# Weight pieces of the MoE experts as halves of one matrix, four rows in one run on each partition; x1, residual and output in natural column order

## The chip, the cores and the metric

The kernel runs on one core of a Trainium2 chip. The metric is the device time of one execution in microseconds (us), the median over several executions. Times below that are not this median come from one profiled execution. The core has TensorE (PE, the matrix products; PEld is its loading of the stationary operand), VectorE (DVE), ScalarE (ACT), GpSimd (POOL) and SyncE (SP), each with its own queue of instructions, and 16 DMA engines that move data between HBM and the on-chip memory SBUF. Products land in PSUM.

## The reference

One decoder layer for 512 tokens of 1024 channels, float32:

```python
mix = hybrid_mixer(x, ...)                        # causal convolution and dilated attention, then W_out
x1  = layer_norm(alpha * x + mix, ln1_g, ln1_b)
# router: top 4 of 32 experts for each token, softmax over the chosen logits
def expert_block(xb, e):
    g = jnp.minimum(xb @ w_gate[e] + b_gate[e], 7.0)
    u = jnp.clip(xb @ w_up[e] + b_up[e], -7.0, 7.0)
    return ((u + 1.0) * g * jax.nn.sigmoid(1.702 * g)) @ w_down[e] + b_down[e]
out = layer_norm(alpha * x1 + sum_of_gated_expert_outputs, ln2_g, ln2_b)
```

Every expert has three matrices of 1024 x 1024 float32 (4 MB each): gate, up and down.

## The kernel before

**Front, 0 to some 262 us.** The mixer, its output projection, the first LayerNorm (LN1) and the router. Its instructions are ordered by a planner (`Plan`): tasks with rough durations and a table of lags are placed one by one on the engine where they can start first. `dma()` of line 410 adds a DMA on SP's queue to that plan. LN1 ends, for each tile `tt` of 128 tokens and each half `hf` of the columns, with a product (line 920) and a sum (line 923), each placed on DVE or POOL, and a store of the tile into `x1d`, a scratch array in HBM.

**Experts, some 272 to 1317 us.** Tokens are gathered by expert. A row is 32 token slots, laid out as four quarters of 256 channels on four groups of 32 partitions. A table (`TURNS`) gives each expert one to four rows: 15 experts have two, 9 have three, 6 have four, 2 have one. For a group of up to four rows, `gather` fetches the rows of `x1d` by an indirect DMA on POOL's queue (`xg`, line 1017), and `xpose` transposes them in blocks of 32 x 32 on DVE into `xT` (shown as `xTg`, line 1053). `expert` then does:

- for pieces c = 0 to 3 of gate and up: for each row, k and quarter q, a product with a stationary `xT` block of 128 x 32 (line 1078, into `gd`); behind the last piece `swiglu` of each row on DVE and ACT (`gm` line 1059, `sg` 1060, `um` 1061 to 1063), ended by the transpose `hT` (line 1064);
- for pieces c = 0, 1 of down: products with `hT`, two rows in one unit with 512 columns (line 1104) where they pair up, else 256 columns (line 1107); the result is split into two parts (lines 1121, 1123) and later summed into `acc` by one-hot products (`combine`, lines 1135 to 1137).

Weights go through a ring of seven places of 2 MB (`wt` six, `wb` one). An expert has six pieces: four with 256 rows of both gate and up (two DMAs of 1 MB, line 302), two with 512 rows of down (one DMA of 2 MB, line 310). `advance()` behind each piece starts the loads for which a place has come free, in program order on SP's queue. The expert numbers behind expert 0 come from `eidi`, cast on POOL behind the first gather (line 1248) and read by SP (line 1155).

Columns stand in a permuted order, in which the quarters interleave by 32: gate, up, x1, the residual sum `acc` and the second LayerNorm are viewed as "(b q c)" with b = 8, q = 4 and c = 32, so that a matmul's moving operand is read in runs of 32 floats.

Of the kernel before, what the change touches and what calls it, by code (L numbers as in the profile page):

```python
# [15 lines left out]
OP = mybir.AluOpType  # L16
# [17 lines left out]
# the blocks of the places, in the order of the main pass: light and heavy ones take turns, as the loads set the pace  # L34
# [15 lines left out]

# column ranges of the constant array
# [28 lines left out]
# how many working buffers the mixer has  # L80
# [10 lines left out]
# how many of a channel's taps the tensor engine makes, and GpSimd adds up  # L91
# [23 lines left out]
class Buf:  # L115
    """Space of one kind: taken when the first task that uses it is placed, given back after the last."""
# [5 lines left out]
class Plan:  # L122
    """The order of a long stretch of instructions: tasks with an engine, a rough duration (us) and what they
    read and write are placed one by one where they can start first; of several, the one with the longest
    path behind it (less its group's lag) goes first. Spaces of a kind are given out in program order; of a bank,
    one engine has to be done before another can begin."""
# [58 lines left out]
    def order(self, lags):  # L185
        """[(start, end, task, engine, {space: place})]"""
# [78 lines left out]
def tile_layer(ctx: ExitStack, tc: tile.TileContext, x, positions, w_in, conv_w, conv_b, conv_ln_g,  # L265
# [22 lines left out]
    def piece():  # L288
        """The next place of the ring, when there is room."""
        i = turn.pop(0)  # L290
        turn.append(i)
        count[0] += 1
        return ring[i].rearrange("p (k a) f -> p k (a f)", a=2)

    def expert_loads(tag, e):
        """The six loads of one expert's weights."""
        def gu_piece(c):
            def f():
                ei = e()
                t = piece().rearrange("p (k g) f -> p k g f", g=2)  # L300
                for gu, src in enumerate((exp_w_gate, exp_w_up)):
                    SP.dma_start(t[:, :, gu], src[0, ei, c * 256:(c + 1) * 256, :].rearrange("e (k p) f -> p (e k) f", p=128))
                got[tag, "gu", c] = t
            return f

        def dn_piece(c):
# [12 lines left out]
    def advance(used=1):  # L319
        """Pieces have been used up: start the loads that now have room."""  # L320
# [27 lines left out]
    # ================= mixer =================  # L348
# [24 lines left out]
    def warm(t, n):  # L373
        """Products that nobody reads: the tensor engine's clock is halved after a pause."""
# [4 lines left out]
    class Late:  # L379
        """Space that another use has had before."""  # L380
# [9 lines left out]
    # Working space in pieces, for the projections and the attention, then taken anew for the second half. Between the  # L390
    # transposes of x and the residual, x's place holds more keys, queries and values.
# [20 lines left out]
    def copy(n, dst, src, r, w, **kw):  # L412
        """A copy that either of two engines can make."""
# [139 lines left out]
    def conv(c):  # L553
        """The first taps as products with diagonal matrices, the next summed by GpSimd, the others added to the products."""
# [46 lines left out]
    def sbuf_tt(o, a, b, opr, r, w, **kw):  # L601
        """An operation on two arrays in SBUF, which either of two engines can make."""
# [8 lines left out]
    # the out projection's operands in upper and lower parts  # L611
# [15 lines left out]
    def pair(c):  # L627
        """q, k, v and the attention of one pair of heads."""
# [23 lines left out]
        def head(tt, h):  # L652
# [6 lines left out]
            # s = -(score / 8 + mask), its least value  # L659
# [221 lines left out]
    for tt in range(TT):  # L881
# [12 lines left out]
        def choose(e, lst=lst, lg=lg, tt=tt):  # L894
            """The four experts of each token."""
# [16 lines left out]
        zv, gv, bv = ((lambda f=f: f().rearrange("p (b q c) -> p q b c", b=8, q=4)) for f in (  # L912
            lambda zn=zn: zn.t(), lnps[0], lnps[1]))
        az = acc[:, tt].rearrange("p (q b c) -> p q b c", b=8, q=4)
# [3 lines left out]
        for hf in range(2):  # L918
            bs = slice(hf * 4, hf * 4 + 4)
            op("VG", (0.6, 1.25), (lambda az, zv, gv, bs: lambda e: (V if e == "V" else G).tensor_tensor(  # L920
                az[:, :, bs], zv()[:, :, bs], gv()[:, :, bs], OP.mult))(az, zv, gv, bs),
               [zn, ("ln", 0)], [("z", tt, 0), ("z", tt, 1), ("x1", tt, hf)])
            op("VG", (0.6, 1.25), (lambda az, bv, bs: lambda e: (V if e == "V" else G).tensor_tensor(
                az[:, :, bs], az[:, :, bs], bv()[:, :, bs], OP.add))(az, bv, bs), [("ln", 1)], [("x1", tt, hf)])
# [15 lines left out]
    # what it takes from here to the first gather  # L940
# [3 lines left out]
    # expert 0's gate and up weights  # L944
# [25 lines left out]
    # ================= experts =================  # L970
# [11 lines left out]
    def hot(members, rank):  # L982
        """One-hot of tokens by slot. Members: (place, first row, rows, first block)."""
# [10 lines left out]
    def by_slot(members, oh, auxp, ps, cols):  # L994
        """Columns of aux by slot."""
# [6 lines left out]
    def by_row(used, ss, ps, cols):  # L1002
        """Columns of ss, each row of slots on all four quarters of the partitions."""
# [4 lines left out]
    def gather(st, sv):  # L1008
        """The rows of x1 that the slots name."""
# [21 lines left out]
    def slots(members, rank, auxp, pool=(sl, "sl")):  # L1031
        """One-hot of tokens by slot; then each slot's token and gate, and the gather of the tokens' rows."""
# [16 lines left out]
    def xpose(st, rows=None):  # L1049
# [3 lines left out]
        V.transpose(st["xT"][:, n].rearrange("p r b t -> p (r b t)"), st["xg"][:, n].rearrange("p r c -> p (r c)"))  # L1053

    def swiglu(st, r, ps):
# [8 lines left out]
        V.transpose(st["hT"][:, r].rearrange("p b t -> p (b t)"), um)  # L1064

    def expert(tag, rows, sel, tick, pool=(gd, "gd"), small=lambda: None, keep=False):
        """rows: (group state, row). Gate and up, SwiGLU, down; tick() runs between the pieces."""
        ps = [pool[0].tile([128, 2, 256], F32, name=pool[1]) for _ in rows]
        bv = bT.rearrange("p g (b q c) -> p g b q c", b=8, q=4)
        for c in range(4):  # L1070
            w = got[tag, "gu", c].rearrange("p k g (b q c) -> p k g b q c", b=8, q=4)
            for i, (st, r) in enumerate(rows):
                if c == 0:
                    for q in range(4):
                        P.matmul(ps[i][q * 32:(q + 1) * 32], sel[0:96], bv[:, :, :, q], start=True, stop=False)
# [484 lines left out]
```

## Time and profile before

| | before |
|---|---|
| time, median of 3 | 1343.4 us (1341.96 to 1344.57) |
| profiled execution, span | 1349.2 us |
| PE busy | 1279.9 us (95%) |
| DVE busy | 680.5 us (50%) |
| ACT busy | 293.8 us (22%) |
| POOL busy | 190.6 us (14%) |
| HBM read | 436.64 MB, 327 GB/s over the span |
| hardware DMA queue | 82.6% of 16 engines' span |

The span runs from the first to the last instruction of the profiled execution; it is 5.8 us above the median time, and stretches of the trace are read against the span. Matmuls are pipelined, and their ends in the trace are modelled, so a PE that is shown as busy need not be at its peak. A float32 matmul leaves two records. In rows of the trace, `out<-in` are the program's names; behind them stand partitions x elements and type; "idle before, releaser" tells how long the engine stood still just before and what ended that.

### The profile page before, as it was taken

How to read it: one execution, taken by the hardware profiler on the slowest of the kernel's cores; microseconds unless marked ns; L12 is line 12 of the kernel's file. 1: busy time of each engine (PE TensorE's matmuls, PEld its weight loads, DVE VectorE, ACT ScalarE, POOL GpSimd, SP SyncE). 2: the span in 40 equal slices, each digit the busy share in tenths (PEclk: the TensorE clock that was granted, in tenths of full speed). 3: DMA queues.
4: the chain of work that ended last, by engine and by line, in shares of the span. 5: the costliest groups of instructions: out<-in, count | busy, mean ns of one | idle time of the engine just before them, and what ended most of it. 6: DMA issues, size and time to landing. Idle time of an engine off the chain costs nothing. (4 is left out here: it accounts for less than half of the span.)

```text
span 1349.2 us, 27298 instructions
## 1 busy us (share of the span) xinstructions
PE 1279.9 (95%) x11407; PEld 578.0 (43%) x11407; DVE 680.5 (50%) x1605; ACT 293.8 (22%) x588; POOL 190.6 (14%) x163
## 2 busy tenths in 40 slices
PE   8989999799999999999999999999999999999993
PEld 7767757533243344433333233435433333433241
DVE  6999764754343443544354343534443543354364
ACT  5677774211011010111010011111110100111022
POOL 2863110511101110101001101010201020000002
PEclk9999999799999999999999999999999999999996
DMA  9400334799999998999999999999999999978991
GB/s 293 145 1 25 105 128 127 291 338 380 406 409 406 406 405 318 379 408 405 405 387 397 405 406 407 386 389 352 403 407 408 349 396 407 371 274 334 397 403 70
DMA packets 126250, 442.72 MB, mean 328 GB/s; under 512 B 8359, under 2 KB 16695, under 8 KB 126124
## 3 DMA queue, kind: packets, MB, share of 16 engines
q1 hardware_dynamic: 122092, 429.98, 82.6%
q0 software_dynamic: 4032, 10.95, 2.4%
q8 instruction: 92, 1.51, 0.5%
q14 instruction: 34, 0.28, 0.1%
HBM read 436.64 MB, written 4.33 MB: 327 GB/s over the span
## 5 line engine op out<-in xcount | busy, mean ns | idle before, releaser
L1078 PE MATMUL gd<-wt,xTg 128*32 128x512 f32 x4592 | 522.7, 593 | 1.4 <-DVE xTg L1053 1.4
L1078 PEld LDWEIGHTS gd<-wt,xTg 128*32 128x32 f32 x4592 | 151.4, 110 | 300.6 <-issue 286.5
L1017 POOL DMA_INDIRECT xg<-x1d,idx x83 | 79.6, 959 | 913.4 <-DVE tk L1046 871.2
L1137 DVE TENSOR_TENSOR acc<-acc,cb 128x512 f32<-128x512 f32 x168 | 107.1, 678 | 181.1 <-PE cb L1136 180.9
L1104 PE MATMUL gd<-wt,hT 128*32 128x512 f32 x1344 | 172.4, 605 | 15.4 <-DVE hT L1064 11.1
L1060 ACT ACTIVATE sg<-gm 128x256 f32<-128x256 f32 x83 | 34.6, 417 | 624.7 <-DVE gm L1059 590.1
L1123 DVE TENSOR_TENSOR yl<-gd,wh 32x256 fp32r<-32x256 f32 (+1 forms) x172 | 86.3, 502 | 131.9 <-ACT wh L1121 130.1
L1121 ACT ACTIVATE wh<-gd 32x256 fp32r<-32x256 f32 (+1 forms) x172 | 75.8, 441 | 274.2 <-PE gd L1104 164.1
L1107 PE MATMUL gd<-wt,hT 128*32 128x256 f32 x1600 | 100.3, 380 | 2.9 <-issue 1.3
L1104 PEld LDWEIGHTS gd<-wt,hT 128*32 128x32 f32 x1344 | 50.1, 111 | 115.1 <-issue 85.9
L1059 DVE TENSOR_SCALAR gm<-gd 128x256 f32<-128x256 f32 x82 | 32.8, 400 | 118.3 <-PE gd L1078 118.3
L546 PE MATMUL bk<-wt,wh 128*128 128x512 f32 (+1 forms) x352 | 80.8, 377 | 1.5 <-ACT wh L415 0.8
L1135 PE MATMUL cb<-wh,cg 128*128 128x512 f32 (+1 forms) x168 | 75.4, 449 | 2.0 <-DVE cg L1129 2.0
L1107 PEld LDWEIGHTS gd<-wt,hT 128*32 128x32 f32 x1600 | 57.9, 110 | 44.4 <-issue 12.1
L1078 PE MATMUL gd<-wb,xTg 128*32 128x512 f32 x656 | 76.6, 593 | 0.0
L546 PEld LDWEIGHTS bk<-wt,wh 128*128 128x128 f32 x352 | 61.0, 189 | 14.6 <-ACT wh L415 1.3
L584 DVE SCALAR_TENSOR_TENSOR bk<-u,cT,bk 128x512 f32<-128x512 f32 x88 | 66.2, 752 | 1.8
L1136 PE MATMUL cb<-yl,cg 128*128 128x512 f32 (+1 forms) x168 | 66.8, 398 | 0.0
L1135 PEld LDWEIGHTS cb<-wh,cg 128*128 128x128 f32 (+1 forms) x168 | 32.0, 190 | 56.6 <-issue 36.3
L1063 DVE SCALAR_TENSOR_TENSOR um<-um,tk,sg 128x256 f32<-128x256 f32 x83 | 42.1, 508 | 9.5
L546 PE MATMUL bk<-wt,wl 128*128 128x512 f32 (+1 forms) x176 | 41.8, 379 | 2.3 <-DVE wl L537 2.1
L1011 DVE TENSOR_REDUCE tk<-sl 128x4 f32<-128x8 f32 (+2 forms) x21 | 3.5, 166 | 77.3 <-PE sl L1005 77.3
(336 smaller groups left out, 1259.9 us busy)
## 6 DMA issues: line engine op xcount, KB each, us to landing
wt<-in_exp_w_gate_dram SPq DMA_DIRECT2D x112, 1024.0 KB
wt<-in_exp_w_up_dram SPq DMA_DIRECT2D x112, 1024.0 KB
wt<-in_exp_w_down_dram SPq DMA_DIRECT2D x52, 2048.0 KB
wb<-in_exp_w_down_dram SPq DMA_DIRECT2D x12, 2048.0 KB
wb<-in_exp_w_gate_dram SPq DMA_DIRECT2D x16, 1024.0 KB
wb<-in_exp_w_up_dram SPq DMA_DIRECT2D x16, 1024.0 KB
wt<-in_w_in_dram SPq DMA_DIRECT2D x3, 2048.0 KB
acc<-in_x_dram SPq DMA_DIRECT2D x8, 512.0 KB
```

The lines of the kernel that those rows point to most:

```text
L546: P.matmul(b.t[:, ts], w.t[:, k], xx[:, k, ts], start=(pas == 0 and k == 0), stop=(pas == 2 and k == KT - 1))
L584: op("V", 0.663, (lambda j: lambda e: V.scalar_tensor_tensor(b.t, u[:, c, j:j + T], cT[:, c, j:j + 1], b.t, op0=OP.mult, op1=OP.add))(j), ...
L1017: G.indirect_dma_start(out=xg[:, r], out_offset=None, in_=x1d[:, :], in_offset=bass.IndirectOffsetOnAxis(ap=idx[:, r:r + 1], axis=0))
L1063: V.scalar_tensor_tensor(um, um, st["tk"][:, 8 + r:9 + r], sg, op0=OP.mult, op1=OP.mult)
L1078: P.matmul(ps[i][q * 32:(q + 1) * 32], st["xT"][:, r, c * 2 + k], w[:, k, :, :, q], start=False, stop=(c == 3 and k == 1))
L1104: P.matmul(d[j * 32:(j + 1) * 32], st["hT"][:, r + j % 2, c * 4 + k], w[:, k, 2 * (j // 2):2 * (j // 2) + 2], **kw)
L1107: P.matmul(d[j * 32:(j + 1) * 32, 0:256], st["hT"][:, r, c * 4 + k], w[:, k, j], **kw)
L1121: S.activation(st["yh"][o], a, AF.Copy)
L1123: V.tensor_tensor(st["yl"][o], a, st["yh"][o].bitcast(F32), OP.subtract)
L1135: P.matmul(ps, cg[0:n, tt * 128:(tt + 1) * 128], st["yh"][0:n, c], start=True, stop=False)
L1136: P.matmul(ps, cg[0:n, tt * 128:(tt + 1) * 128], st["yl"][0:n, c], start=False, stop=True)
L1137: V.tensor_tensor(acc[:, tt, c], acc[:, tt, c], ps, OP.add)
```

## The change

1. A piece of gate or up weights is now a half (512 rows) of one matrix, as a down piece was before: gate first half, up first half, gate second half, up second half, then the two halves of down, each by one DMA of 2 MB. The rows are taken "(p k)": partition p gets rows 4p to 4p + 3 as one run of 16 KB, where it got runs of 4 KB.
2. A gate/up piece then has four k blocks of one matrix instead of two of both; a product has 256 columns and goes to the gate or the up part of `gd`, and there are twice as many.
3. As the channels are handed to partitions in a new order, the two DVE transposes read their source at steps of four floats (16 bytes) instead of contiguously.
4. x1, `acc`, biases and the second LayerNorm are in natural column order. A tile's store into `x1d` becomes two stores of 256 KB, one for each half of the columns, in runs of 512 bytes.

```diff
 def expert_loads(tag, e):
-    def gu_piece(c):
-        def f():
-            ei = e()
-            t = piece().rearrange("p (k g) f -> p k g f", g=2)
-            for gu, src in enumerate((exp_w_gate, exp_w_up)):
-                SP.dma_start(t[:, :, gu], src[0, ei, c * 256:(c + 1) * 256, :].rearrange("e (k p) f -> p (e k) f", p=128))
-            got[tag, "gu", c] = t
-        return f
...
+    def half(src, kind, c, h):
+        def f():
             ei = e()
             t = piece()
-            SP.dma_start(t, exp_w_down[0, ei, c * 512:(c + 1) * 512, :].rearrange(
-                "e (k p) f -> p (e k) f", p=128))
-            got[tag, "dn", c] = t
+            SP.dma_start(t.rearrange("p k f -> p (k f)"),
+                         src[0, ei, h * 512:(h + 1) * 512, :].rearrange("e (p k) f -> p (e k f)", k=4))
+            got[tag, kind, c] = t
         return f
-    return [gu_piece(c) for c in range(4)] + [dn_piece(c) for c in range(2)]
+    return [half((exp_w_gate, exp_w_up)[c % 2], "gu", c, c // 2) for c in range(4)] + [
+        half(exp_w_down, "dn", h, h) for h in range(2)]
...
-    stores.append(("x1d", tt))
-    dma(524288, x1d[tt * 512:(tt + 1) * 512, :].rearrange("(p q) c -> p (q c)", q=4), acc[:, tt], r=[("x1", tt, hf) for hf in range(2)], w=[("x1d", tt)])
+    stores.extend(("x1d", tt, hf) for hf in range(2))
+    for hf in range(2):
+        dma(262144, x1d[tt * 512:(tt + 1) * 512, hf * 128:(hf + 1) * 128].rearrange("(p q) j -> p q j", q=4),
+            acc[:, tt, hf * 512:(hf + 1) * 512].rearrange("p (q j) -> p q j", q=4), r=[("x1", tt, hf)],
+            w=[("x1d", tt, hf)])
...
 def xpose(st, rows=None):
-    V.transpose(st["xT"][:, n].rearrange("p r b t -> p (r b t)"), st["xg"][:, n].rearrange("p r c -> p (r c)"))
+    V.transpose(st["xT"][:, n].rearrange("p r b t -> p (r b t)"),
+                st["xg"][:, n].rearrange("p r (h c k) -> p (r h) k c", h=2, k=4))
...
 def swiglu(st, r, ps):
-    V.transpose(st["hT"][:, r].rearrange("p b t -> p (b t)"), um)
+    V.transpose(st["hT"][:, r].rearrange("p b t -> p (b t)"), um.rearrange("p (h c k) -> p h k c", h=2, k=4))
...
 def expert(tag, rows, sel, tick, pool=(gd, "gd"), small=lambda: None, keep=False):
-        w = got[tag, "gu", c].rearrange("p k g (b q c) -> p k g b q c", b=8, q=4)
+        h, g = divmod(c, 2)
+        w = got[tag, "gu", c].rearrange("p k (h q j) -> p k q h j", h=2, q=4)
...
-            for k in range(2):
+            for k in range(4):
                 for q in range(4):
-                    P.matmul(ps[i][q * 32:(q + 1) * 32], st["xT"][:, r, c * 2 + k], w[:, k, :, :, q], start=False,
-                             stop=(c == 3 and k == 1))
+                    P.matmul(ps[i][q * 32:(q + 1) * 32, g], st["xT"][:, r, h * 4 + k], w[:, k, q], start=False,
+                             stop=(c == 3 and k == 3))
...
-        w = got[tag, "dn", c].rearrange("p k (b q c) -> p k q b c", b=8, q=4)
+        w = got[tag, "dn", c]
...
-                             w[:, k, 2 * (j // 2):2 * (j // 2) + 2], **kw)
+                             w[:, k, j // 2 * 512:j // 2 * 512 + 512], **kw)
...
-                        P.matmul(d[j * 32:(j + 1) * 32, 0:256], st["hT"][:, r, c * 4 + k], w[:, k, j], **kw)
+                        P.matmul(d[j * 32:(j + 1) * 32, 0:256], st["hT"][:, r, c * 4 + k],
+                                 w[:, k, j * 256:(j + 1) * 256], **kw)
```

The order of instructions on SP, where the front ends and expert 0's last weights are loaded, before (line, operation, out<-in, shape, how many in a run):

```order
L302 DMA wt_1788<-in_exp_w_gate_dram 128x2x1024
L302 DMA wt_1788<-in_exp_w_up_dram 128x2x1024
L302 DMA wt_1841<-in_exp_w_gate_dram 128x2x1024
L302 DMA wt_1841<-in_exp_w_up_dram 128x2x1024
L410 DMA x1d<-acc 128x1024 x2
L310 DMA wt_1922<-in_exp_w_down_dram 128x4x1024
L410 DMA x1d<-acc 128x1024 x2
L310 DMA wt_1979<-in_exp_w_down_dram 128x4x1024
L1155 TENSOR_LOAD eidi
```

The same place on SP in the changed kernel:

```order
L302 DMA wt_1786<-in_exp_w_gate_dram 128x4096
L302 DMA wt_1838<-in_exp_w_up_dram 128x4096
L403 DMA x1d<-acc 512x1x128 x3
L302 DMA wt_1916<-in_exp_w_down_dram 128x4096
L403 DMA x1d<-acc 512x1x128 x4
L302 DMA wt_1978<-in_exp_w_down_dram 128x4096
L403 DMA x1d<-acc 512x1x128
L1154 TENSOR_LOAD eidi
```

All stores stood ahead of the second down load; now the last of the eight stands behind it. The first gather on POOL waits for all stores in both kernels.

On PE, the end of the gate and up pieces and the start of the down pieces of an expert with three rows, before (`gd` is the result in PSUM, `sl` that of small products of another group):

```order
L1078 MATMUL gd<-wt_1922,xTg 32x512 x24
L1005 LDWEIGHTS rows_1999
L1005 MATMUL sl<-ss,rows_1999 128x5
...
L1078 MATMUL gd<-wt_1979,xTg 32x512 x24
L1078 MATMUL gd<-wb_1986,xTg 32x512 x24
L1107 MATMUL gd<-wt_70,hT 32x256 x16
L1104 MATMUL gd<-wt_70,hT 32x512 x16
```

The same place on PE in the changed kernel:

```order
L1076 MATMUL gd<-wt_1916,xTg 32x256 x48
L1000 LDWEIGHTS rows_1999
L1000 MATMUL sl<-ss,rows_1999 128x5
...
L1076 MATMUL gd<-wt_1978,xTg 32x256 x48
L1076 MATMUL gd<-wb_1986,xTg 32x256 x48
L1105 MATMUL gd<-wt_70,hT 32x256 x16
L1102 MATMUL gd<-wt_70,hT 32x512 x16
```

Nothing stands elsewhere; each run of gate and up products has twice the instructions at half the columns. Apart from line numbers and shapes the order on DVE, ACT and POOL is the same in both.

## Rows read from the trace of the kernel before

**Rows 1.** the page's first part: busy time of TensorE over the span

```profile
span 1349.2 us, 27298 instructions
...
PE 1279.9 (95%) x11407; PEld 578.0 (43%) x11407; DVE 680.5 (50%) x1605; ACT 293.8 (22%) x588; POOL 190.6 (14%) x163
```

**Rows 2.** busy time by stages: stretch, length, each engine, granted clock, DMA share, GB/s

```profile
262.00:275.00 13.00, 9.43 (x67) 3.32 (x70) 9.70 (x52) 5.28 (x6) 3.88 (x5) 0.64 0.81 277
275.00:1300.00 1025.00, 1004.74 (x9941) 376.40 (x9933) 441.57 (x1123) 114.15 (x260) 76.14 (x80) 1.00 0.99 386
```

**Rows 3.** the same view, two slices of 25 us of the experts' pass

```profile
800.00:825.00 25.00, 24.06 (x296) 9.43 (x292) 11.51 (x31) 3.84 (x10) 0.00 (x0) 1.00 1.03 408
1175.00:1200.00 25.00, 25.00 (x248) 9.10 (x240) 12.38 (x30) 1.67 (x4) 2.85 (x3) 1.00 0.75 279
```

**Rows 4.** line 1078: min/median/max ns, first and last start; what ended PE's waits

```profile
L1078 PE MATMUL gd<-wb,xTg x656: 590/592/617, 308.0 to 1115.8; 128*32 128x512 f32 x164
L1078 PEldq EVENT_SEMAPHORE  x128: 51/51/51, 267.7 to 1307.9; - x128
...
L1078 PE MATMUL sl<-wt,xTg x64: 590/592/617, 1297.5 to 1311.7; 128*32 128x512 f32 x64
...
  DMA wt<-in_exp_w_gate_dram: 0.6, 2
```

**Rows 5.** line 1064 (hT), and who waited for it (us, times)

```profile
L1064 DVE STREAM_TRANSPOSE hT<-um x83: 445/445/447, 294.8 to 1327.2; 128x256 f32<-128x256 f32 x83
...
  PEld gd L1104: 26.3, 17
  PE gd L1104: 12.4, 13
  PEld gd L1107: 4.0, 7
```

**Rows 6.** timeline of an expert with two rows: start, us, engine, line

```profile
324.25 0.42 DVE L1059 TENSOR_SCALAR gm<-gd 128x256 f32<-128x256 f32 x1
...
328.27 0.45 DVE L1064 STREAM_TRANSPOSE hT<-um 128x256 f32<-128x256 f32 x1
...
328.77 1.06 PE L1104 MATMUL gd<-wt,hT 128*32 128x512 f32 x8 [1.01 <-DVE hT L1064]
```

**Rows 7.** timeline of TensorE alone, 799 to 832 us

```profile
802.01 3.62 PE L1078 MATMUL gd<-wb,xTg 128*32 128x512 f32 x32
805.44 7.05 PE L1078 MATMUL gd<-wt,xTg 128*32 128x512 f32 x64
...
815.37 5.39 PE L1107 MATMUL gd<-wt,hT 128*32 128x256 f32 x96 [0.20 <-DVE hT L1064]
820.57 0.40 PE L1075 MATMUL gd<-wl,selr 96*32 96x512 bf16 x4
```

**Rows 8.** the costliest groups of the page: busy us, mean ns, idle before

```profile
L1078 PE MATMUL gd<-wt,xTg 128*32 128x512 f32 x4592 | 522.7, 593 | 1.4 <-DVE xTg L1053 1.4
...
L1107 PE MATMUL gd<-wt,hT 128*32 128x256 f32 x1600 | 100.3, 380 | 2.9 <-issue 1.3
```

**Rows 9.** transposes xTg of whole groups, by line and shape: busy us, mean ns

```profile
L1053 DVE STREAM_TRANSPOSE xTg<-xg 128x1024 f32<-128x1024 f32 x19 | 23.2, 1219 | 0.4 <-DMA xg<-x1d,idx 0.4
```

**Rows 10.** timeline, a reduction that reads at steps of 128 bytes

```profile
269.78 1.07 DVE L1261 TENSOR_REDUCE Gf<-hT 128x128 f32<-128x512 f32 x1
```

**Rows 11.** timeline before the experts' pass; SPq is SyncE's queue, with its waits

```profile
254.76 7.76 SPq L410 DMA_DIRECT2D x1d<-acc  x2
...
266.46 1.16 POOL L1017 DMA_INDIRECT xg<-x1d,idx  x1 [4.28 <-DVE wl L1227]
...
272.31 0.45 DVE L1053 STREAM_TRANSPOSE xTg<-xg 128x256 f32<-128x256 f32 x1 [1.21 <-DMA xg<-x1d,idx]
...
272.81 1.92 PE L1078 MATMUL gd<-wt,xTg 128*32 128x512 f32 x16 [1.37 <-DVE xTg L1053]
```

**Rows 12.** DMA issues from 246 to 276 us, KB each, median us to landing

```profile
xg<-x1d,idx POOLq DMA_INDIRECT x3, 5.2
```

More of the change, by code (lines that the diff above doesn't have):

```diff
@@ L295, in expert_loads @@
     def expert_loads(tag, e):
-        def gu_piece(c):
-            def f():
-                ei = e()
-                t = piece().rearrange("p (k g) f -> p k g f", g=2)
-                for gu, src in enumerate((exp_w_gate, exp_w_up)):
-                    SP.dma_start(t[:, :, gu], src[0, ei, c * 256:(c + 1) * 256, :].rearrange("e (k p) f -> p (e k) f", p=128))
-                got[tag, "gu", c] = t
-            return f
-        def dn_piece(c):
+        def half(src, kind, c, h):
             def f():
@@ L911, in tile_layer @@
         zn = buf("zn")
-        zv, gv, bv = ((lambda f=f: f().rearrange("p (b q c) -> p q b c", b=8, q=4)) for f in (
-            lambda zn=zn: zn.t(), lnps[0], lnps[1]))
-        az = acc[:, tt].rearrange("p (q b c) -> p q b c", b=8, q=4)
+        zv, gv, bv = (lambda zn=zn: zn.t()), lnps[0], lnps[1]
+        az = acc[:, tt]
         op("A", 1.13, (lambda tt, lst, zn: lambda e: S.activation(
@@ L918, in tile_layer @@
         for hf in range(2):
-            bs = slice(hf * 4, hf * 4 + 4)
+            bs = slice(hf * 512, hf * 512 + 512)
             op("VG", (0.6, 1.25), (lambda az, zv, gv, bs: lambda e: (V if e == "V" else G).tensor_tensor(
-                az[:, :, bs], zv()[:, :, bs], gv()[:, :, bs], OP.mult))(az, zv, gv, bs),
+                az[:, bs], zv()[:, bs], gv()[:, bs], OP.mult))(az, zv, gv, bs),
                [zn, ("ln", 0)], [("z", tt, 0), ("z", tt, 1), ("x1", tt, hf)])
             op("VG", (0.6, 1.25), (lambda az, bv, bs: lambda e: (V if e == "V" else G).tensor_tensor(
-                az[:, :, bs], az[:, :, bs], bv()[:, :, bs], OP.add))(az, bv, bs), [("ln", 1)], [("x1", tt, hf)])
-        stores.append(("x1d", tt))
-        dma(524288, x1d[tt * 512:(tt + 1) * 512, :].rearrange("(p q) c -> p (q c)", q=4), acc[:, tt], r=[("x1", tt, hf) for hf in range(2)], w=[("x1d", tt)])
+                az[:, bs], az[:, bs], bv()[:, bs], OP.add))(az, bv, bs), [("ln", 1)], [("x1", tt, hf)])
+        stores.extend(("x1d", tt, hf) for hf in range(2))
[3 more added lines that the diff above has]
+                w=[("x1d", tt, hf)])
     pl.group = "rank0"
@@ L1063, in swiglu @@
         V.scalar_tensor_tensor(um, um, st["tk"][:, 8 + r:9 + r], sg, op0=OP.mult, op1=OP.mult)
-        V.transpose(st["hT"][:, r].rearrange("p b t -> p (b t)"), um)
+        V.transpose(st["hT"][:, r].rearrange("p b t -> p (b t)"), um.rearrange("p (h c k) -> p h k c", h=2, k=4))
     def expert(tag, rows, sel, tick, pool=(gd, "gd"), small=lambda: None, keep=False):
         ps = [pool[0].tile([128, 2, 256], F32, name=pool[1]) for _ in rows]
-        bv = bT.rearrange("p g (b q c) -> p g b q c", b=8, q=4)
+        bv = bT.rearrange("p g (h q j) -> p q g h j", h=2, q=4)
         for c in range(4):
-            w = got[tag, "gu", c].rearrange("p k g (b q c) -> p k g b q c", b=8, q=4)
+            h, g = divmod(c, 2)
+            w = got[tag, "gu", c].rearrange("p k (h q j) -> p k q h j", h=2, q=4)
             for i, (st, r) in enumerate(rows):
@@ L1074, in expert @@
                     for q in range(4):
-                        P.matmul(ps[i][q * 32:(q + 1) * 32], sel[0:96], bv[:, :, :, q], start=True, stop=False)
-                for k in range(2):
+                        P.matmul(ps[i][q * 32:(q + 1) * 32], sel[0:96], bv[:, q], start=True, stop=False)
+                for k in range(4):
                     for q in range(4):
-                        P.matmul(ps[i][q * 32:(q + 1) * 32], st["xT"][:, r, c * 2 + k], w[:, k, :, :, q], start=False,
-                                 stop=(c == 3 and k == 1))
+                        P.matmul(ps[i][q * 32:(q + 1) * 32, g], st["xT"][:, r, h * 4 + k], w[:, k, q], start=False,
+                                 stop=(c == 3 and k == 3))
                 if c:
@@ L1314, in add_bias @@
         V.tensor_copy(GT[0:NE], ps[0:NE])
-        bdp = t[0:NE, 0].rearrange("p (b q c) -> p q b c", b=8, q=4)
         yield
@@ L1319, in add_bias @@
                 ps = cb.tile([128, 512], F32, name="cb")
-                P.matmul(ps, GT[0:NE, tt * 128:(tt + 1) * 128], bdp[:, 2 * hf:2 * hf + 2], start=True, stop=True)
+                P.matmul(ps, GT[0:NE, tt * 128:(tt + 1) * 128], t[0:NE, 0, hf * 512:(hf + 1) * 512], start=True,
+                         stop=True)
                 c = slice(hf * 512, (hf + 1) * 512)
@@ L1417, in outputs @@
         g2, b2 = (got["last"][:, i] for i in range(2))
-        gv = g2.rearrange("p (b q c) -> p q b c", b=8, q=4)
         zn = [None] * TT
@@ L1428, in outputs @@
                 o = mw.tile([128, D], F32, name=("yl", "yl", "xTg", "hT")[tt - 1])
-                V.tensor_tensor(o.rearrange("p (b q c) -> p q b c", b=8, q=4),
-                                zn[tt - 1].rearrange("p (q b c) -> p q b c", q=4, b=8), gv, OP.mult)
+                V.tensor_tensor(o, zn[tt - 1], g2, OP.mult)
                 G.tensor_tensor(o, o, b2, OP.add)
@@ L1441, in outputs @@
             qs = slice(q * 32, (q + 1) * 32)
-            S.activation(gl_[qs].rearrange("p (b c) -> p b c", b=8), quarter(got["last"][:, 0], q), AF.Copy)
+            S.activation(gl_[qs], quarter(got["last"][:, 0], q), AF.Copy)
         yield
     def quarter(t, q):
-        return t[q * 32:(q + 1) * 32].rearrange("p (b q c) -> p q b c", b=8, q=4)[:, q]
+        return t[q * 32:(q + 1) * 32, q * 256:(q + 1) * 256]
     def last_rows():
@@ L1462, in last_rows @@
             qs = slice(q * 32, (q + 1) * 32)
-            V.scalar_tensor_tensor(ol[0:32].rearrange("p (b q c) -> p q b c", b=8, q=4)[:, q],
-                                   zl[qs].rearrange("p (b c) -> p b c", b=8), st[qs, 14:15], quarter(got["last"][:, 1], q),
+            V.scalar_tensor_tensor(ol[0:32, q * 256:(q + 1) * 256], zl[qs], st[qs, 14:15], quarter(got["last"][:, 1], q),
                                    op0=OP.mult, op1=OP.add)
```

## The prediction

> **What bounds the kernel now.** I first read the shares of the page: TensorE (PE) is busy for 1279.9 of 1349.2 us, 95% [rows 1]. That is an average, so I cut the span by stages. The experts' pass, 275 to 1300 us, is three quarters of it, and there PE is busy for 1004.74 of 1025 us at full clock, while the DMA engines are busy for 0.99 of the time at 386 GB/s [rows 2]. Two resources look full, and which of them is waited for has to be read elsewhere. In two slices of 25 us the reader can tell them apart: from 800 to 825 us DMA is full (1.03, 408 GB/s), but from 1175 to 1200 us it falls to 0.75 and 279 GB/s while PE is still at 25.00 of 25 [rows 3]. So the ring of weight places was full and the loads waited for PE, not the other way. The gate and up products say the same: all their waits for gate weights in ring places "wt" come to 0.6 us in two instances [rows 4]. Whatever makes the loads faster therefore finds almost nothing to remove. What PE does wait for is VectorE's (DVE's) last step of SwiGLU, the transpose hT of line 1064: weight loads of the down products waited for it 17 times (26.3 us) and 7 times (4.0 us) [rows 5]. One such place in full: the first gm starts at 324.25, the second row's hT at 328.27 takes 0.45 us, and PE goes on at 328.77 after 1.01 us idle [rows 6]. Whatever lengthens this chain lengthens the kernel.
>
> **The change part by part.** (1) *Loads.* 32 experts times 6 pieces of 2.1 MB are the same bytes; only runs (4 KB to 16 KB) and instructions differ (two DMAs per gate/up piece become one). At 408 GB/s [rows 3] the 402.7 MB take 987 us, less than the pass of 1025 us. I cost this at 0: PE's work covers it. If the cover were gone, a few per cent of the rate would be worth 10 us or more; that is a rival below. Each gate/up piece also loses the wait for its second DMA, of which PE's queue recorded 128, 51 ns each [rows 4]: 6.5 us if all lay on the path, 0 if the queue runs ahead of the array. PE's pieces follow each other without a gap [rows 7], so 0.
>
> (2) *Gate and up products in 256 columns instead of 512.* Each product is two records in the trace (float32), and line 1078 has 4592 + 656 + 64 = 5312 records of 512 columns [rows 4, 8]; they become 10624 of 256. The pace of 512: from 802.01 to 805.44 us 32 records, 107.2 ns each. That of 256 is shown by line 1107, the down products of single rows: from 815.37 to 820.57 us 96 records, 54.2 ns each [rows 7]. Two of them are 108.4 ns, 1.2 ns more than one of 512, and 5312 x 1.2 = 6.4 us. The starts are rounded to 10 ns and a change of line lies within both stretches, so I take **+5 us**, with bounds 0 (the array does the same columns) and +8.5 (1.6 ns each). The average over the groups looks worse: 100.3 us / 1600 = 62.7 ns against 522.7 / 4592 = 113.8 ns [rows 8]; by these it would be (2 x 62.7 - 113.8) x 5312 = +62 us. I don't take it, because most groups of line 1107 are short and their busy time holds the drain of the last product and waits inside; the run of 96 is the undisturbed one. [...]
>
> (3) *Transposes that read with a step of 16 bytes.* The rows of a weight piece now lie four to a partition, so channels must be handed out in the same order, and both transposes read every fourth float. Contiguous, hT takes 445 ns for 256 elements [rows 5], and the 1024 elements of xTg 1219 ns [rows 9]: 1.01 ns an element and 0.19 us besides. The trace has no transpose with a step. The nearest row that reads floats with one is the reduction of line 1261, 512 floats at steps of 128 bytes: 1.07 us [rows 10], where the contiguous rate would give 0.19 + 512 x 1.01 = 0.71. That is 0.70 ns more an element, 0.18 us for 256. Bounds: 0 if the step costs nothing, 0.26 us if the rate is halved (256 x 1.01 ns). I take **0.18 us**, by the nearest row, though it is of another operation. How often does it show? At each of the 24 waits [rows 5] PE stands at the end of a chain that DVE works off row by row, with mostly two transposes in it: 24 x 2 x 0.18 = 8.6 us. Places where PE isn't kept waiting now, with four rows, stay covered. So **+9 us**, bounds 0 and 24 x 2 x 0.26 = 12.5. The 19 transposes xTg of whole groups become 4 x 0.18 = 0.7 us longer, 14 us in all if PE waited for each; they are made an expert ahead and DVE is busy for only 441.57 of 1025 us [rows 2], so 0. [...]
>
> (4) *The stores of x1 and the first gather.* Before, SP has issued the last two stores at 262.52 us (254.76 + 7.76, most of it waiting for their data), and the 2 MB load of down weights follows them; the gather, which needs the stores alone, goes out at 266.46 [rows 11]. In the changed order the last of eight stores stands behind that load, and the gather needs it. 2.1 MB at 408 GB/s are 5.1 us: from about 263.5 to 268.6, the store of 256 KB in short runs about 1 us more and its completion another 1 or so, hence 270.7 instead of 266.46, 4.2 us late. But the gathers now took a median of 5.2 us to land [rows 12], beside the same load, and would have the DMA engines to themselves; if they need 3 to 5 us, xTg comes 2 to 4 us later than at 272.31. PE's first gate product, now at 272.81, follows it [rows 11]. [...] I take 3 us for the delay and 1 for the clock, **+4 us**, with bounds 0 (the gather's faster landing gives all back) and +6. Queued behind the late gather on POOL is the cast of the expert numbers, for which SP's next weight loads wait; the first piece so loaded, in a ring place "wb", is used at 308.0 us [rows 4], some 35 us after the pass begins, which covers them.
>
> (5) *Natural order elsewhere*: additions and scalings run over whole rows, same element counts; 0, perhaps -0.5 us in the tail.
>
> Sum: 5 + 9 + 4 = +18 us; 1349.2 becomes 1367. The profiled execution is 5.8 us above the median of 1343.4, so the median becomes **1361 us**.
>
> **Rivals.** *The step costs nothing* (no row of a transpose speaks against it): 5 + 4 = +9, 1352 us. *The loads set the pace after all*, which ends on the other side: DMA stands at 1.03 in many slices [rows 3], so the longer runs and single waits could start PE's pieces earlier. PE's idle time in the pass is 1025 - 1004.74 = 20.3 us, of which 12.4 end with hT before line 1104 [rows 5]; if the other 8 and the 6.5 us of second waits went, with the transposes free, the sum is 5 + 4 - 14.5 = -5.5, 1338 us. It decides from the point where more than 9 us of PE's pace hang on loads; 0.6 us of waits speak against it [rows 4]. *Issue bounds the short products*: +62 by the averages of [rows 8], and 9 + 4 more, about 1418 us; the undisturbed run of [rows 7] speaks against it. [...] *Nothing shows*: the gather's landing gives the delay back, the array takes the same columns, the transposes are free: 1343.
>
> **How the numbers follow.** Forecast 0.55 (its own range 1350 to 1372, from its bounds), free step 0.20, loads 0.12, nothing 0.08, issue 0.05. Below 1339 lies a little over half of the loads' chance, above 1374 the issue's and a little of the forecast's, so the range is 1339 to 1374. A measurement of this kernel can tell about 0.2%, 2.7 us, from no change. Slower are the first two and the last, 0.80, less 0.08 for their low ends: 0.72. Same: 0.08 and 0.05 of those, 0.13. Faster: 0.12 and 0.03, 0.15.
>
> **What would show it.** hT at about 0.62 us instead of 0.445, and waits of down weight loads for it up by about 9 us; xTg at 1.9; runs of 256-column products at 54 ns a record; the first gather out near 270.7 and the first gate product near 275.8; no more waits for weights than now. The prediction is wrong if hT stays at 0.445, if the gate products' pace rises to 60 ns, or if PE's idle time falls.

## The result, and the profile after

The changed kernel takes 1362.54 us (median of 4 runs, 1361.69 to 1366.64) against 1343.8 us for the kernel before: 1.0145 times as long, 95% interval 1.0128 to 1.0162. Forecast were 1361 us and "slower".

The first part of the page of the changed kernel, its costliest line, and its row on the loading of instructions:

```profile
span 1359.9 us, 37410 instructions
...
PE 1286.0 (95%) x16719; PEld 749.5 (55%) x16719; DVE 715.7 (53%) x1605; ACT 293.7 (22%) x588; POOL 189.7 (14%) x163
...
q8 instruction: 133, 2.18, 0.6%
...
L1076 PE MATMUL gd<-wt,xTg 128*32 128x256 f32 x9184 | 528.1, 380 | 5.9 <-DVE xTg L1048 5.9
```

PE is still the engine that is full. Stages of the changed kernel (length, busy time of PE, PEld, DVE, ACT and POOL, granted clock, DMA share, GB/s), which answer to [rows 2]:

```profile
262.00:275.00 13.00, 7.30 (x43) 2.51 (x42) 7.13 (x39) 4.26 (x6) 1.31 (x2) 0.63 0.67 224
275.00:285.00 10.00, 7.67 (x104) 3.90 (x108) 3.47 (x14) 1.13 (x1) 2.12 (x3) 0.66 0.68 246
275.00:1300.00 1025.00, 1003.21 (x15113) 541.98 (x15113) 471.05 (x1119) 111.47 (x254) 78.01 (x83) 1.00 0.94 383
```

In the pass the DMA share fell from 0.99 to 0.94 at nearly the same rate (383 GB/s, before 386): the loads became cheaper, and PE's share didn't move (1003.21 us busy, before 1004.74). In the slices of the two pages in which the loads run freely, the engines move 421 to 428 GB/s, where they moved 405 to 409. The transposes hT in the changed kernel, and who waited for them, which answers to [rows 5]:

```profile
L1061 DVE STREAM_TRANSPOSE hT<-um x83: 625/645/674, 301.3 to 1337.7; 128x256 f32<-128x256 f32 x83
...
  PEld gd L1102: 31.5, 22
  PE gd L1102: 14.9, 14
  PEld gd L1105: 5.3, 8
```

hT went from 0.445 to 0.645 us; PE's weight loads now wait for it 30 times, 36.8 us, where it was 24 times, 30.3 us, in the profile of [rows 5]. The first experiment below gives the count with contiguous transposes on a chip like that of the result: 21 times, 25.3 us. The transposes xTg of whole groups, which answer to [rows 9]:

```profile
L1048 DVE STREAM_TRANSPOSE xTg<-xg 128x1024 f32<-128x1024 f32 x19 | 39.9, 2101 | 3.9 <-DMA xg<-x1d,idx 3.9
```

They take 2.10 us instead of 1.22, 0.86 ns more an element; hT's 0.200 us is 0.78 ns an element. PE's timeline at the place of [rows 7]:

```profile
808.26 3.64 PE L1076 MATMUL gd<-wb,xTg 128*32 128x256 f32 x64
811.71 7.09 PE L1076 MATMUL gd<-wt,xTg 128*32 128x256 f32 x128
...
822.04 5.39 PE L1105 MATMUL gd<-wt,hT 128*32 128x256 f32 x96 [0.39 <-DVE hT L1061]
827.24 0.40 PE L1073 MATMUL gd<-wl,selr 96*32 96x512 bf16 x4
```

From 808.26 to 811.71 us 64 records of 256 columns pass, 53.9 ns each; two of them are 107.8 ns, where one of 512 was 107.2. At last the place before the pass, which answers to [rows 11]:

```profile
263.20 0.34 SPq L302 DMA_DIRECT2D wt<-in_exp_w_down_dram  x1
...
263.61 0.53 SPq L403 DMA_DIRECT2D x1d<-acc  x1
...
273.62 1.15 POOL L1012 DMA_INDIRECT xg<-x1d,idx  x1 [11.47 <-DMA x1d<-acc]
...
276.64 0.63 DVE L1048 STREAM_TRANSPOSE xTg<-xg 128x256 f32<-128x256 f32 x1 [5.57 <-DMA xg<-x1d,idx]
...
277.32 0.20 PEld L1076 LDWEIGHTS gd<-wt,xTg 128*32 128x32 f32 x8 [6.37 <-DVE xTg L1048]
```

The last store is issued behind the down load, POOL's gather waits for that store until 273.62, 7.2 us later than before, and PE starts the gate products at 277.32, 4.5 us later. The clock of 0.66 from 275 to 285 us (above) says that it started at the lower level: by single microseconds it is 0.50 from 275 to 281 us and 1.00 from 282 us on. What the DMA engines moved meanwhile, in steps of 2 us (GB/s last):

```profile
264.00:266.00 2.00, 1.45 (x18) 0.66 (x18) 1.54 (x15) 0.00 (x0) 0.00 (x0) 0.50 1.08 300
266.00:268.00 2.00, 1.90 (x9) 0.67 (x9) 1.38 (x13) 0.00 (x0) 0.00 (x0) 0.50 1.03 410
268.00:270.00 2.00, 2.00 (x6) 0.75 (x5) 1.58 (x7) 1.85 (x3) 0.00 (x0) 0.50 0.93 348
270.00:272.00 2.00, 1.46 (x7) 0.12 (x5) 1.04 (x2) 0.26 (x1) 0.00 (x0) 0.63 0.54 175
```

### The profile page after: what moved, and what is told of

The parts are those of the page before. It is cut to its first block, busy times and chain, and to the rows that moved or that the text cites. A ratio compares the mean times of both kernels' runs of the same rounds, so it can differ in the third digit from the quotient of the medians.

```text
span 1359.9 us, 37410 instructions
## 1 busy us (share of the span) xinstructions
PE 1286.0 (95%) x16719; PEld 749.5 (55%) x16719; DVE 715.7 (53%) x1605; ACT 293.7 (22%) x588; POOL 189.7 (14%) x163
## 5 line engine op out<-in xcount | busy, mean ns | idle before, releaser
L1076 PE MATMUL gd<-wt,xTg 128*32 128x256 f32 x9184 | 528.1, 380 | 5.9 <-DVE xTg L1048 5.9
L1076 PEld LDWEIGHTS gd<-wt,xTg 128*32 128x32 f32 x9184 | 305.5, 110 | 202.8 <-issue 18.9
L1102 PEld LDWEIGHTS gd<-wt,hT 128*32 128x32 f32 x1344 | 48.5, 110 | 113.2 <-issue 76.1
L1105 PE MATMUL gd<-wt,hT 128*32 128x256 f32 x1600 | 104.0, 380 | 4.2 <-DVE hT L1061 1.7
L1105 PEld LDWEIGHTS gd<-wt,hT 128*32 128x32 f32 x1600 | 56.0, 110 | 47.2 <-issue 10.7
L1076 PE MATMUL gd<-wb,xTg 128*32 128x256 f32 x1312 | 77.6, 379 | 0.0
L1076 PEld LDWEIGHTS gd<-wb,xTg 128*32 128x32 f32 x1312 | 45.3, 110 | 26.9 <-issue 2.2
L1061 DVE STREAM_TRANSPOSE hT<-um 128x256 f32<-128x256 f32 x83 | 53.8, 648 | 2.9
L1048 DVE STREAM_TRANSPOSE xTg<-xg 128x1024 f32<-128x1024 f32 (+2 forms) x24 | 44.1, 1839 | 10.0 <-DMA xg<-x1d,idx 9.9
```

The source lines that it names most:

```text
L1076: P.matmul(ps[i][q * 32:(q + 1) * 32, g], st["xT"][:, r, h * 4 + k], w[:, k, q], start=False, stop=(c == 3 and k == 3))
L1105: P.matmul(d[j * 32:(j + 1) * 32, 0:256], st["hT"][:, r, c * 4 + k], w[:, k, j * 256:(j + 1) * 256], **kw)
```

## The experiments

The twelve runs were made in three sets, each on one chip, with the kernel before timed beside them: it took 1342.8 us in the first set, 1350.9 us in the second and 1351.8 us in the third. That difference between chips is part of what was found, so every ratio is to the kernel before of the same set. The 1.0145 of the whole change was measured apart from these sets, beside a kernel before of 1343.8 us, and is set against the ratios of the first.

**First set. Both transposes contiguous** in the changed kernel (channels then meet other weight rows):

```diff
-    V.transpose(st["xT"][:, n].rearrange("p r b t -> p (r b t)"),
-                    st["xg"][:, n].rearrange("p r (h c k) -> p (r h) k c", h=2, k=4))
+    V.transpose(st["xT"][:, n].rearrange("p r b t -> p (r b t)"), st["xg"][:, n].rearrange("p r c -> p (r c)"))
...
-    V.transpose(st["hT"][:, r].rearrange("p b t -> p (b t)"), um.rearrange("p (h c k) -> p h k c", h=2, k=4))
+    V.transpose(st["hT"][:, r].rearrange("p b t -> p (b t)"), um)
```

> The changed kernel with both transposes (xTg and hT) reading contiguously again; channels then meet the wrong weight rows, so its output is another function of the same size of work. Theory of the prediction (the step of 16 bytes costs about 9 us through the waits for hT): hT back at 445 ns, the time about 9 us under the changed kernel, near 1353 to 1354 us, 1.007 times the kernel before. Rival (hT's extra time is hidden, and the 256-column products or the loads cost the time): hT back at 445 ns, but the time stays within 2 us of the changed kernel's 1362.5.

Measured: 1351.64 us, ratio 1.0069 (1.0055 to 1.0084); against the 1.0145 of the whole change that is 0.76%, 10.2 us, give or take 3 us by the two intervals. hT in this run and its waits:

```profile
L1060 DVE STREAM_TRANSPOSE hT<-um x83: 445/445/447, 300.3 to 1325.7; 128x256 f32<-128x256 f32 x83
...
  PEld gd L1101: 22.8, 15
...
  PEld gd L1104: 2.5, 6
```

The step of 16 bytes is the largest term, and the rival that hides it falls. With the step the waits grow from 25.3 to 36.8 us.

**Stores ahead of the load** in the changed kernel:

```diff
-        stores.extend(("x1d", tt, hf) for hf in range(2))
-        for hf in range(2):
-            dma(262144, x1d[tt * 512:(tt + 1) * 512, hf * 128:(hf + 1) * 128].rearrange("(p q) j -> p q j", q=4),
-                acc[:, tt, hf * 512:(hf + 1) * 512].rearrange("p (q j) -> p q j", q=4), r=[("x1", tt, hf)],
-                w=[("x1d", tt, hf)])
+        stores.append(("x1d", tt))
+        op("D", 524288 / 359e3, (lambda tt: lambda e: [SP.dma_start(
+            x1d[tt * 512:(tt + 1) * 512, hf * 128:(hf + 1) * 128].rearrange("(p q) j -> p q j", q=4),
+            acc[:, tt, hf * 512:(hf + 1) * 512].rearrange("p (q j) -> p q j", q=4)) for hf in range(2)])(tt),
+           [("x1", tt, hf) for hf in range(2)], [("x1d", tt)])
```

> The changed kernel, with the two half stores of a tile put into SP's queue together, when both halves are ready, so that all eight stand ahead of the second down load again. Theory (the store behind the load delays the first gather, and PE then starts at the lower clock): the gather goes out near 266.5 us instead of 273.6, the first gate product starts near 272.8 to 273 instead of 277.3, no stretch at the lower clock behind it, and the time falls by 5 to 7 us to about 1356. Rival (the gather is late for another reason, such as the runs of 512 bytes, or the ring makes up for it later): less than 2 us.

Measured: 1355.47 us, ratio 1.0089 (1.0076 to 1.0103), 0.56% or 7.5 us, give or take 3, under the whole change. Its timeline at the same place, and two of its stretches:

```profile
266.70 1.15 POOL L1012 DMA_INDIRECT xg<-x1d,idx  x1 [4.07 <-DVE wl L1226]
...
272.47 0.63 DVE L1048 STREAM_TRANSPOSE xTg<-xg 128x256 f32<-128x256 f32 x1 [0.88 <-DMA xg<-x1d,idx]
...
273.16 0.20 PEld L1076 LDWEIGHTS gd<-wt,xTg 128*32 128x32 f32 x8 [2.71 <-DVE xTg L1048]
```

```profile
274.00:276.00 2.00, 2.00 (x24) 0.99 (x20) 1.80 (x11) 0.00 (x0) 0.00 (x0) 0.50 1.01 434
276.00:278.00 2.00, 2.00 (x40) 1.06 (x36) 0.00 (x0) 0.00 (x0) 0.00 (x0) 0.98 0.92 393
```

The gather leaves within 0.3 us of the time before and PE starts within 0.4 us, though the stores still have runs of 512 bytes: the place in SP's queue made the delay. One part of the expectation failed: the clock is at 0.50 from 274 to 276 us, so the pass starts at the lower level here too, only for a shorter time than in the changed kernel.

**256-column products alone**, in the kernel before:

```diff
-                for k in range(2):
-                    for q in range(4):
-                        P.matmul(ps[i][q * 32:(q + 1) * 32], st["xT"][:, r, c * 2 + k], w[:, k, :, :, q], start=False,
-                                 stop=(c == 3 and k == 1))
+                for g in range(2):
+                    for k in range(2):
+                        for q in range(4):
+                            P.matmul(ps[i][q * 32:(q + 1) * 32, g], st["xT"][:, r, c * 2 + k], w[:, k, g, :, q], start=False,
+                                     stop=(c == 3 and k == 1 and g == 1))
```

> The kernel before, with each gate and up product of 512 columns split into one of 256 for gate and one for up; loads, order of columns, transposes and stores as before. Theory of the prediction (two products of 256 are a little slower than one of 512): +3 to +8 us, near 1348. Rival 1 (the array does the same columns in the same time): within 2 us of before, 1343.8. Rival 2 (issue of short products bounds, by the averages of the groups): +60 us.

Measured: 1346.06 us, ratio 1.0023 (1.0011 to 1.0035): +3.1 us (1.5 to 4.7 by the interval), at the low end of the theory. By the time alone rival 1, with its 2 us, isn't excluded; the pace decides with it: 107.8 instead of 107.2 ns for the same columns, times 5312, is 3.2 us.

**The kernel before once more.**

> The kernel before, unchanged, profiled once more. Its first profile had two places, at 354 and 750 us, where gm came 1.5 us late, PE stood idle and the granted clock then fell to half for some 3.4 us; the profile of the changed kernel has neither. If they belong to that one execution: a span near 1343 to 1345 us without them, the time 1343.8. If they belong to the kernel: both places again, a span near 1349.

Measured: 1343.21 us, ratio 1.0008 (0.9997 to 1.0020), the profiled span 1339.8 us, less even than expected. The first gm of the expert near 350 us in this run:

```profile
350.55 0.42 DVE L1059 TENSOR_SCALAR gm<-gd 128x256 f32<-128x256 f32 x1 [4.61 <-PE gd L1078]
```

It waits 4.61 us for PE; in the profile that the prediction was made from the same wait was 6.03 us, and after it the clock fell to 0.50 (357 to 360 us). So the two places are not always there. The second set shows where they belong.

**Second set, another chip. hT's step alone**, in the kernel before:

```diff
-        V.transpose(st["hT"][:, r].rearrange("p b t -> p (b t)"), um)
+        V.transpose(st["hT"][:, r].rearrange("p b t -> p (b t)"), um.rearrange("p (h c k) -> p h k c", h=2, k=4))
```

> The kernel before, with the transpose hT alone reading at a step of 16 bytes (channels then meet the wrong rows of the down weights, so its output is another function of the same size of work); xTg stays contiguous. Theory (hT's step acts through the waits for hT): hT at 0.64 to 0.65 us, +0.37 us for each expert of two rows behind its gate and up products, about 10 us in all, near 1353 us; the 1 us or so that is left of the 11 between the changed kernel and the one with both transposes contiguous belongs to xTg. Rival (xTg is late and takes most of it): less than 5 us.

Measured: 1362.13 us against 1350.91, ratio 1.0086 (1.0068 to 1.0104), +11.2 us. hT and its waits, and the first gm of the same expert as above:

```profile
L1064 DVE STREAM_TRANSPOSE hT<-um x83: 625/642/679, 295.9 to 1338.6; 128x256 f32<-128x256 f32 x83
...
  PEld gd L1104: 33.7, 22
...
  PEld gd L1107: 6.9, 11
```

```profile
353.58 0.42 DVE L1059 TENSOR_SCALAR gm<-gd 128x256 f32<-128x256 f32 x1 [6.06 <-PE gd L1078]
```

hT alone makes the whole term, as far as the intervals tell (11.2 give or take 2.4 here, 10.2 give or take 3 for both transposes). And the late gm is here again, 6.06 us, on a chip on which the kernel before takes 1350.9 us. The profile that the prediction was made from has both marks, the span of 1349.2 us and the late gm, so it was probably taken on such a chip, and the timed runs, 1343.4 us, on one of the other kind; that is argued from these marks.

**The order of channels made by the products**, with hT contiguous and the stores ahead of the load:

```diff
-            w = got[tag, "gu", c].rearrange("p k (h q j) -> p k q h j", h=2, q=4)
+            w = got[tag, "gu", c].rearrange("p b (h q c k) -> p b q h k c", h=2, q=4, k=4)
```

> The changed kernel with the stores ahead of the load (as in the second experiment), and with the order of channels made by the gate and up products instead of by hT: their moving operand is read at a step of 16 bytes, and hT reads contiguously; the output is the reference's. Theory 1 (TensorE reads its moving operand at any step at the same pace): hT at 445 ns, products at 54 ns a record, the time near 1346, like the kernel before with 256-column products. Theory 2 (TensorE pays for the step as VectorE does): the pace of these products rises, at half rate by up to 570 us, and the time lies far above 1362.

Measured: 1977.09 us, ratio 1.4634 (1.4613 to 1.4655). PE's timeline:

```profile
801.05 3.88 PE L1076 MATMUL gd<-wt,xTg 128*32 128x256 f32 x32
804.71 0.28 PE L994 MATMUL sl<-aux,oh 128*32 128x5 bf16 x15
```

32 records take 3.66 us, 114 ns each instead of 54. Theory 2 holds: with TensorE's moving operand at a step of 16 bytes the products go at less than half the pace, and there it hits the engine that is full.

**Contiguous transposes and early stores; more products that nobody reads** (20 more behind the 7 of the start):

```diff
-    warm(wm, WARM1[2])
+    warm(wm, WARM1[2] + 20)
```

> The changed kernel with both transposes contiguous (another output, as in the first experiment) and the stores ahead of the load: what is left of the change is the loads of 16 KB runs, one DMA a piece, and the products of 256 columns. Theory (loads are hidden behind TensorE): the time of the kernel before with 256-column products, 1346 us within 2 us. Rival (the longer runs and the missing second waits give time back): 1343 or less.

> The changed kernel with 20 more products that nobody reads while TensorE waits for the first gather. Theory (part of the late start's cost is that TensorE begins the pass at the lower clock, some 4 us of it): the granted clock is at full from 277 us on, and the time falls by about 2 us, to 1360. Rival (the clock costs nothing there): within 1 us of the changed kernel.

Measured: 1380.6 us, ratio 1.0220 (1.0205 to 1.0236), and 1397.79 us, ratio 1.0340 (1.0325 to 1.0355). Neither theory had room for such times. Both kernels have the 256-column products, and their traces show PE idle in the middle of runs of gate products with "issue" as the cause. In the pass of the first of the two (us in total, times, longest):

```profile
PE gd L1075 <- issue: 14.9, 28, 0.8
```

The third set follows this up.

**Third set, a third chip, of the slower kind.**

> The kernel before with 256-column gate and up products, once more, on whichever chip this set runs. In the set with hT's step alone the kernel before took 1350.9 us and the kernels with 256-column products had stalls inside runs of gate and up products that nothing in the trace ends; in the set before it 1342.8 us and no such stalls. Theory I (twice the instructions on TensorE's queue bring the stalls, where the chip is slow to supply them): where the kernel before takes about 1351, this one has them too, at +20 us or more; where it takes about 1343, +3 us as before. Rival L (the loads of 16 KB runs bring them): +3 us on either.

Measured: 1385.88 us, ratio 1.0251 (1.0237 to 1.0265): +34 us for the edit that cost 3 us on the first chip. PE's timeline in one run of gate products of this run; then what PE itself waited for in its pass (us in total, times, longest):

```profile
419.74 4.50 PE L1079 MATMUL gd<-wt,xTg 128*32 128x256 f32 x74
425.04 0.64 PE L1079 MATMUL gd<-wt,xTg 128*32 128x256 f32 x4 [0.80 <-issue]
426.46 1.24 PE L1079 MATMUL gd<-wt,xTg 128*32 128x256 f32 x17 [0.78 <-issue]
```

```profile
PE gd L1079 <- issue: 15.5, 28, 0.8
```

In the first set's run of the same kernel such a run passes whole:

```profile
411.59 5.39 PE L1079 MATMUL gd<-wt,xTg 128*32 128x256 f32 x96
```

Of the instructions of line 1079 (these products), what ended the idle time of PE and of its weight loads together (us, times), in this run and, in the last fence, in the first set's run:

```profile
  issue: 68.3, 122
...
  DMA wt<-in_exp_w_gate_dram: 2.5, 7
```

```profile
  issue: 20.5, 58
```

Within one run of products PE stands still twice for 0.8 us, and "issue" says that the trace shows nothing that it waits for. The sums of 68.3 and 20.5 us hold weight loads that wait while PE is busy; PE's own idle time for this reason is 15.5 us here, and the first set's run has none for these products. The last experiment below, with 512 columns on this same chip, has none either. That is still too little, as a record is shown for 0.38 us and the next one starts 0.05 us behind it on average, so the start of a stop is hidden. The starts of the records show it all: behind the slow start of the pass there are 36 places in this run where the next gate or up product starts 0.46 to 1.19 us after the one before, 29.8 us together, and none in the first set's run. That is most of the 31 us between +34 and +3. Between the stops the mean pace is nearly the same, 53.1 against 52.4 ns a record. Loads, transposes and stores are those of the kernel before. Theory I stands in so far as the stops come with this edit, which doubles both the products and the loads of the stationary operand; the runs don't tell these two apart.

Why PE then stops is open. That it waits for its instructions to be brought would fit the row of instruction loads, 133 of 16 KB each in the changed kernel where the kernel before has 92:

```profile
q8 instruction: 92, 1.51, 0.5%
```

But it is argued and not shown, and two readings of the traces don't support it: the loads took as long on the first chip as on this one (median 1.08 and 1.07 us), and in 31 of the 36 stops none of them lands.

> The changed kernel with both transposes contiguous (another output) and the stores ahead of the load, once more. On a chip without the stalls (the kernel before at about 1343): the time of the kernel before with 256-column products, about 1346, within 2 us, if loads are hidden; 1343 or less if the longer runs give time back. With the stalls (the kernel before at about 1351): theory I, the same time as the kernel before with 256-column products; rival L, some 25 us more than that.

Measured: 1379.07 us, ratio 1.0202 (1.0188 to 1.0216): 6.8 us less than the 256-column products with the old loads, where theory I had the same time. Part of it lies ahead of the pass, as the gate products start at 272.0 instead of 274.5 us, and the 2.5 us of waits for gate weights above are gone. The two kernels differ in the order of columns and in the stores as well as in the loads, so what the loads give back isn't shown. Rival L falls: the loads don't bring the stops.

> The changed kernel with 20 more products that nobody reads, once more. On a chip without the stalls: 2 us less than the changed kernel's 1362.5 if the lower clock at the start of the pass costs time, 1362.5 if it doesn't. With the stalls: about 1398 as in the set before.

Measured: 1397.21 us, ratio 1.0338 (1.0324 to 1.0352). The time says nothing on the start, as the stops drown it; the row shows the clock:

```profile
275.00:285.00 10.00, 8.71 (x134) 4.66 (x135) 3.52 (x14) 2.30 (x3) 3.07 (x4) 1.00 0.56 197
```

With PE kept at work (the 27 products are shown from 269.05 to 276.87 us) the clock is at 1.00 from 275 to 285 us, where the changed kernel had 0.66. What that is worth in time was not measured on a chip without the stops.

> The kernel before, with hT reading at a step of two floats (8 bytes) instead of contiguously (channels then meet the wrong rows of the down weights, so the output is another function of the same size of work). [...] Rival (any step costs): hT at 0.55 to 0.65 us and 5 to 10 us more.

The edit is that of hT's step alone with k = 2, h = 4. Measured: 1350.8 us against 1351.77, ratio 0.9995 (0.9986 to 1.0005). hT:

```profile
L1064 DVE STREAM_TRANSPOSE hT<-um x83: 445/445/447, 298.7 to 1330.9; 128x256 f32<-128x256 f32 x83
```

At a step of 8 bytes hT takes 445 ns, as it does contiguously; at one of 16 it took 642 ns (the run of hT's step alone). The rival, in which any step costs, falls; why the step of 16 bytes costs and that of 8 doesn't, no run shows. The first gm of the expert near 350 us waits 6.04 us for PE here, so the late gm is on this chip too.

## Why the prediction was right, step by step

The time (1361 against 1362.5) and its sign were right, and so were the three mechanisms that were priced. By ratios of the first chip they cost 3.1 (products), 10.2 (transposes) and 7.5 us (stores), forecast were 5, 9 and 4. They make 20.8 us, and 1.0145 is 19.5; each of the two larger is known to 3 us only, so the 1.3 us between the sums say nothing. That the sum came within 1.5 us is in part luck: one term was too large and two were too small.

1. *Loads, 0*: right in kind. They became cheaper (DMA share 0.94 for 0.99), and in the changed kernel the gate and up products have no wait for weights left (before it was 0.6 us for gate weights in places "wt"). The rival in which loads set the pace fell with the sign. No run has the loads alone on a chip without the stops; what is left beside the three terms there is 1.3 us, give or take 4.
2. *Products, +5*: 3.1 on the first chip; the pace of 53.9 ns a record is the row that was chosen, not the average of [rows 8]. The rival "issue bounds the short products" didn't happen there. On the third chip the same edit costs 34 us, not by a slower pace, as the rival had it, but by stops within a run; the prediction had no term for these.
3. *Transposes, +9*: 10.2. The borrowed price of line 1261, 0.70 ns an element, was 0.78 for hT and 0.86 for xTg, as luck would have it not far off, for it is of another operation. The 24 waits came from a profile of the slower kind of chip; on the first chip there are 21 with contiguous transposes, and the changed kernel has 30, as places that were covered came into the open. The waits grew by 11.5 us, which agrees with the 10.2 of the time. That xTg is hidden agrees with the runs: hT alone makes 11.2 on its chip.
4. *Stores and gather, +4*: the mechanism was right and the size too small, 7.5. The gather left at 273.62, not 270.7: the sum had the load and the last store pass in 6.1 us from 263.5, and by the rows above the queue moved 2.47 MB, about their bytes, from 264 to 272 us, at 308 GB/s on average instead of 408. That left the gather 1.6 us behind, near the 1 us that the sum had for the store's completion, an estimate for which there is no row; no run shows it alone. That it then lands sooner, 2.7 us instead of 5.2, was foreseen as 3 to 5. The row:

```profile
xg<-x1d,idx POOLq DMA_INDIRECT x3, 2.7
```

No run shows the sum's 1 us for the clock: the start at the lower clock is in the rows, but its share of the 7.5 us was not measured alone. What they show is that the changed kernel's first 32 records of 256 columns, at 0.50, take from 277.32 to 280.74 us, 106.9 ns each, where later ones take 53.9. An estimate from the rows: 0.66 from 275 to 285 us is 6.8 us at 0.50, of which PE worked from 277.32 on, some 4.5 us, and lost half, 2.2 us. With the stores ahead of the load PE works at the lower level from 273.16 to about 276 us and loses some 1.4. The later start (4.2 us) and this difference make 5 of the 7.5 us, within the interval.

5. *The base*: 1349.2 was probably a span of the slower kind of chip, by the marks above, and the difference of 5.8 us to the median was not an offset of the profile, as the sum took it: the profiled execution of the changed kernel took 1361.69 us with a span of 1359.9, 1.8 us less. The span of the kernel before on the first chip is 1339.8. The sum came out because a difference was added to the median in the end.

## What to carry to other kernels

Before a layout for longer DMA runs is paid for with a step, look whether anything waits for the loads, and who reads at that step: a step of 16 bytes between float32 elements made the VectorE transposes 45% (hT) and 72% (xTg) longer and cost a TensorE moving operand more than half its pace (114 ns a record, 54 without the step); 8 bytes cost the transpose hT nothing (445 ns), so two rows a partition would be the layout to try first (not tried as a whole). A store that a gather needs should not stand behind a 2 MB load in the same queue: here that cost 7.5 us. Halving the columns of a matmul doubles its instructions, which cost 3 us on one chip and 34 on another; time it on more than one.

## What was not expected of the hardware

The same program, the one with 256-column products, took 1346.06 and 1385.88 us on two chips, and the kernel before 1342.8 and 1351.8. Most of the first difference is PE standing still inside runs of products; why is open. So is why gm starts 1.4 us late on the slower kind (at two places, after waits of 6.03 and 6.04 us, in the profile that the prediction was made from; the first set's run has 4.61 us at the first of them). None of the versions that were run is faster than the kernel before.
